# Column-tiled ones-matmuls with a split partial sum for the norm sums of an eight-core decoder trunk

## The chip, the cores and the metric

The kernel runs on all eight cores of one Trainium2 chip: two dies of four cores. Every core works on its own prompt sequence of 2048 tokens and on 16 of the 128 sample tokens, with the same weights. The metric is the device time of the slowest core in microseconds (us). TensorE does the matmuls, VectorE and ScalarE the elementwise work; in the traces each engine goes through its own instructions in the program's order (TensorE's matmuls match the program one for one), and the engines wait for each other by semaphores. SBUF ("MEM" in the profile) is the core's memory, PSUM ("PS") is where TensorE writes: 128 partitions, eight banks of 512 fp32 columns.

Executions of this program come in two states. In the slow one a die shows a lower granted TensorE clock (the share of full speed that the profile says TensorE was given) and the time is some per cent, at most 19%, longer.

## The reference, cut to what matters

```python
def rmsnorm(x, g):
    xf = x.astype(jnp.float32)
    y = xf * lax.rsqrt(jnp.mean(xf * xf, axis=-1, keepdims=True) + EPS)
    return (y * g.astype(jnp.float32)).astype(x.dtype)

def trunk(...):                                    # two layers
    for i in range(DEPTH):
        u = rmsnorm(x, g_mix[i])
        x = x + (pool_mixer(u, ...) if i % 2 == 0 else conv_mixer(u, ...))
        x = x + mem_attend(rmsnorm(x, g_attn[i]), mem_k[i], mem_v[i], w_q[i], w_o[i])
        x = x + sq_relu_mlp(rmsnorm(x, g_ffn[i]), w_up[i], w_down[i])
    return rmsnorm(x, g_final), ...
```

D_MODEL is 1024 and D_FF 4096. The change touches the sum of x*x over 1024 channels in the norms named g_attn, g_ffn and in g_mix of layer 1 (the samples' own 16-column g_ffn sums excepted).

## The kernel before: the parts that matter

Activations lie transposed: channels on the 128 partitions (8 chunks of 128), tokens along the columns. The 2064 tokens of a core are five tiles: four of 416 columns and one of 400 (384 prompt tokens and the 16 samples; without the samples 384 in some stages). A sum over channels is a sum over partitions, which TensorE does with a matrix of ones: eight matmuls, one per channel chunk, accumulate in one PSUM bank, and every row of the bank then holds the full sum.

```python
def norm_r(ti, U, RSTD, n=None):                   # U holds the squares, bf16
    bk = nxt()                                     # next PSUM bank, in rotation
    for c in range(NCH):                           # NCH = 8, ONESB is 128 x 128 ones
        mm(PSv(bk, 0, n), ONESB(), U(c, sl(0, n)), c == 0, c == NCH - 1)
    act(PSv(bk, 0, n), PSv(bk, 0, n), AF.Ln, scale=1.0 / D, bias=EPS)    # ScalarE
    act(RSTD(sl(0, n)), PSv(bk, 0, n), AF.Exp, scale=-0.5)

def norm_s(...):                                   # "gain products", VectorE, eight of them
    for c in cs:
        stt(U(c, ...), X(c, ...), G(c, ...), RSTD(...), ALU.mult, ALU.mult)
```

The helper `norm_b` is `norm_r` followed by `norm_s`. The program has 25 such norms: 1 in the prelude, 6 in each attention phase, 4 and 3 in the two MLPs, 5 in the conv phase. They are put between the chunks of the main work (a chunk is eight matmuls of one tile, 1.41 us at 416 columns), so that ScalarE and VectorE make the next tile's input while TensorE is at this one. The attention phase:

```python
def S(k, mid):                                     # scores of tile k
    for m in range(8):
        bk = nxt()
        ...8 matmuls into bk...
        act(pt(m), PSv(bk, 0, n), AF.Exp, scale=1.0 / 16.0)
        if m % 2 == 1 and m > 1:
            den(m // 2 - 1)                        # a bank, 2 matmuls, Ln, Exp, two products on VectorE
        mid(m)
    den(3)

def O(k, mid):                                     # output of tile k
    for ec in range(8):
        bk = nxt()
        ...8 matmuls into bk, which read pt...
        tt(X(ec, ...), PSv(bk, 0, n), X(ec, ...), ALU.add)
        mid(ec)

def SA(b):                                         # one sample's scores: "dots"
    for h2 in range(2):
        bk = nxt()
        mm(PSv(bk, 0, 512), ..., QS(...), True, True)
        for x in range(2):
            for hh in range(2):
                dot(kv, kv, PSv(bk, hh * 256, (hh + 1) * 256), SS(...))   # VectorE, 0.42 us each

# where things stand in S(k), k > 0 (and in the last O)
if m == 2:  N2b(k + 1) if k + 1 < NT else N3b(0)   # the next norm
if m == 5:  step()                                 # SB: 8 column-tiled matmuls; then SA
if ec == 5: N3b(1)
```

S(k) is followed by O(k-1), and a second sample's step stands at O's chunk ec == 3. Banks rotate over seven in these phases (bank 7 holds the samples' output). Count `nxt()` from SA on: SA takes two banks; chunks m = 6 and 7, den(2), den(3) and ec = 0 take the other five; so O's second and third chunk (ec = 1 and 2) write the two banks that the dots read. They may start only when four, or all eight, of the dots are done.

The softmax here doesn't subtract the row's maximum and nothing guards it: scores larger than these inputs give would overflow.

## Time and profile before

| | before |
|---|---|
| time, median of 3 runs | 1623.22 us (1622.68 to 1623.79) |
| TensorE busy | 1575.0 us, 97% of the span |
| VectorE, ScalarE busy | 854.2 us (53%), 560.8 us (35%) |
| granted TensorE clock | 0.99 |
| norm sums on TensorE | 25 x eight matmuls, 34.8 us |

The first lines are from the profile's page of the kernel before (its slowest core): busy time by engine; the chain of waits that ended last, by engine and by line; and groups of instructions, each with `out<-in` and shape, count, busy us, mean ns of one, then the engine's idle us just before them and what ended most of it. L292 is the plain matmul helper, L327 the helper of the gain products, L304 that of the dots.

```profile
PE 1575.0 (97%) x10104; PEld 906.3 (56%) x10104; DVE 854.2 (53%) x1907; ACT 560.8 (35%) x1054; POOL 113.9 (7%) x245
PE 92%; DVE 2%; ACT 2%; DMA 2%; issue 2%; POOL 0%; DVEq 0%; ACTq 0%; SPq 0%; POOLq 0%
PE PS L292 89%; PE PS L296 2%; DVE MEM L327 1%; ACT MEM L319 1%; PE PS L301 1%; DMA MEM<-gv 1%; DMA MEM<-x 1%; ACT MEM L308 1%; DVE MEM L331 0%; DVE MEM L345 0%; DVE MEM L339 0%; POOL MEM L354 0%; ACT MEM L343 0%; DVEq L1389 0%; ACTq L1389 
L292 PE MATMUL PS<-MEM 128*128 128x416 bf16 (+7 forms) x9024 | 1501.3, 327 | 8.3 <-DVE MEM L345 2.7
L327 DVE SCALAR_TENSOR_TENSOR MEM<-MEM 128x416 bf16<-128x416 f32 (+7 forms) x322 | 176.9, 601 | 126.9 <-ACT MEM L319 108.5
L304 DVE SCALAR_TENSOR_TENSOR MEM<-MEM,PS 128x256 f32<-128x256 f32 x256 | 105.2, 420 | 72.0 <-PE PS L292 49.0
```

TensorE is the limit: 97% busy, 92% of the chain, and before 9024 matmuls it idles 8.3 us in all. VectorE is only half busy *on average*. The next view is VectorE's timeline in one attention tile of layer 1 (core 5; start us, duration us, instruction, count, and in brackets the idle time before it with its cause; the short accumulator reads between the dots are left out).

```profile
1071.76 4.59 DVE L327 SCALAR_TENSOR_TENSOR MEM<-MEM 128x416 bf16<-128x416 f32 x8 [6.28 <-ACT MEM L319]
1076.27 2.09 DVE L331 TENSOR_TENSOR MEM<-MEM 128x416 bf16<-128x416 bf16 x4
1078.27 0.41 DVE L304 SCALAR_TENSOR_TENSOR MEM<-MEM,PS 128x256 f32<-128x256 f32 x1
...
1079.94 0.42 DVE L304 SCALAR_TENSOR_TENSOR MEM<-MEM,PS 128x256 f32<-128x256 f32 x1
...
1081.89 0.42 DVE L304 SCALAR_TENSOR_TENSOR MEM<-MEM,PS 128x256 f32<-128x256 f32 x1
1082.45 2.10 DVE L331 TENSOR_TENSOR MEM<-MEM 128x416 bf16<-128x416 bf16 x4
```

From 1071.76 to 1086 us VectorE hardly rests (no gap is over 0.2 us): eight gain products (4.59 us), four products by a softmax denominator (2.09), eight dots (1078.27 to 1082.31), and so on. So in this stretch it is not half busy, it is full. The same stretch of TensorE, kernel before:

```profile
1075.62 4.05 PE L292 MATMUL PS<-MEM 16*128 16x512 bf16 x21
1079.90 5.96 PE L292 MATMUL PS<-MEM 128*128 128x416 bf16 x33 [0.23 <-ACT MEM L319]
1085.80 0.40 PE L296 MATMUL PS<-MEM 128*16 128x257 bf16 x8
```

The run of 33 matmuls from 1079.90 is the last denominator matmul and O's first four chunks, without a stop. Its third chunk starts 17 matmuls of 176 ns after 1079.90, at 1082.89 us, and the dots that free its bank end at 1082.31. That is a margin of 0.58 us.

The kernel already has column-tiled matmuls, those of SB, each with 16 rows of output. This is their group in the view of groups kept apart by shape, TensorE, kernel before:

```profile
L296 PE MATMUL PS<-MEM 128*16 128x257 bf16 x256 | 12.7, 275 | 2.1 <-ACT MEM L319 2.1
```

### The profile page before, as it was taken

The numbers are of one execution on the slowest core, as the hardware profiler recorded it, in microseconds if no ns is written. First come the engines' busy times: TensorE is split into PE (matmuls) and PEld (weight loads), VectorE is DVE, ScalarE is ACT, GpSimd is POOL, SyncE is SP. The second block draws the span as 40 slices with busy tenths as digits, with TensorE's granted clock in tenths as the row PEclk, the third lists the DMA queues.
The fourth block names the chain that finished last, engine by engine and source line by source line (L and its number), as shares of the span: only waits on it lengthen the run. The fifth ranks groups of instructions, "written<-read, shape, count | busy, mean of one in ns | idle before, by whom it ended". The sixth has DMA issues, their size and how long they took to land.

```text
span 1624.3 us, 28431 instructions; the slowest of 8 cores (1618.2 to 1624.3 us)
## 1 busy us (share of the span) xinstructions
PE 1575.0 (97%) x10104; PEld 906.3 (56%) x10104; DVE 854.2 (53%) x1907; ACT 560.8 (35%) x1054; POOL 113.9 (7%) x245
## 2 busy tenths in 40 slices
PE   4899999999999999999999999999999999999997
PEld 3775555555555556555555555555555555555565
DVE  5666675655444444445666665766455444442235
ACT  4756344541122222222133224433643112213453
POOL 2002121110000000000000001121010000000000
PEclk8899999999999999999999999999999999999999
DMA  9978793575537516066000009694654663000012
GB/s 228 208 116 156 161 183 68 122 148 77 85 66 126 107 24 105 1 104 109 1 1 1 1 1 151 130 201 96 126 118 68 101 105 52 14 1 1 40 64 108
DMA packets 84565, 145.13 MB, mean 89 GB/s; under 512 B 4286, under 2 KB 37310, under 8 KB 84412
## 3 DMA queue, kind: packets, MB, share of 16 engines
q0 software_dynamic: 67568, 84.08, 35.4%
q1 hardware_dynamic: 16860, 59.24, 10.6%
q8 instruction: 84, 1.38, 0.3%
q14 instruction: 53, 0.43, 0.1%
HBM read 212.42 MB, written 14.36 MB: 140 GB/s over the span
## 4 chain that ended last, share of the span: by engine, by line
PE 92%; DVE 2%; ACT 2%; DMA 2%; issue 2%; POOL 0%; DVEq 0%; ACTq 0%; SPq 0%; POOLq 0%
PE PS L292 89%; PE PS L296 2%; DVE MEM L327 1%; ACT MEM L319 1%; PE PS L301 1%; DMA MEM<-gv 1%; DMA MEM<-x 1%; ACT MEM L308 1%; DVE MEM L331 0%; DVE MEM L345 0%; DVE MEM L339 0%; POOL MEM L354 0%; ACT MEM L343 0%; DVEq L1389 0%; ACTq L1389 0%
## 5 line engine op out<-in xcount | busy, mean ns | idle before, releaser
L292 PE MATMUL PS<-MEM 128*128 128x416 bf16 (+7 forms) x9024 | 1501.3, 327 | 8.3 <-DVE MEM L345 2.7
L292 PEld LDWEIGHTS PS<-MEM 128*128 128x128 bf16 (+1 forms) x9024 | 837.3, 98 | 659.8 <-issue 38.5
L319 ACT ACTIVATE MEM<-PS 128x416 f32<-128x416 f32 (+5 forms) x469 | 238.9, 510 | 632.5 <-PE PS L292 622.7
L331 DVE TENSOR_TENSOR MEM<-PS,MEM 128x416 f32<-128x416 f32 (+6 forms) x533 | 297.8, 575 | 264.2 <-PE PS L292 256.1
L331 DVE TENSOR_TENSOR MEM<-MEM 128x416 bf16<-128x416 f32 (+3 forms) x282 | 159.9, 584 | 198.8 <-ACT MEM L319 189.5
L327 DVE SCALAR_TENSOR_TENSOR MEM<-MEM 128x416 bf16<-128x416 f32 (+7 forms) x322 | 176.9, 601 | 126.9 <-ACT MEM L319 108.5
L319 ACT ACTIVATE MEM<-MEM 128x416 bf16<-128x416 f32 (+9 forms) x299 | 185.2, 631 | 146.5 <-DVE MEM L331 111.6
L304 DVE SCALAR_TENSOR_TENSOR MEM<-MEM,PS 128x256 f32<-128x256 f32 x256 | 105.2, 420 | 72.0 <-PE PS L292 49.0
L343 ACT COPY MEM<-PS 128x512 f32<-128x512 f32 (+3 forms) x73 | 39.2, 536 | 129.5 <-PE PS L292 119.1
L296 PE MATMUL PS<-MEM 128*128 128x128 bf16 (+4 forms) x896 | 61.0, 248 | 16.3 <-DVE MEM L339 9.4
L296 PEld LDWEIGHTS PS<-MEM 128*128 128x128 bf16 (+2 forms) x896 | 49.2, 107 | 30.2 <-issue 28.6
L343 ACT CAST MEM<-PS 128x512 bf16<-128x512 f32 (+2 forms) x65 | 35.2, 554 | 68.0 <-PE PS L292 67.3
L345 DVE CAST MEM<-PS 128x512 bf16<-128x512 f32 (+1 forms) x76 | 48.5, 658 | 11.7 <-PE PS L292 11.7
L354 POOL DMA_DIRECT2D MEM<-cv x64 | 47.7, 745 | 13.4 <-PE PS L292 13.4
L319 ACT ACTIVATE PS<-PS 128x416 f32<-128x416 f32 (+3 forms) x67 | 33.2, 495 | 41.5 <-PE PS L292 41.1
L327 DVE SCALAR_TENSOR_TENSOR MEM<-PS,MEM 128x1024 f32<-128x1024 f32 (+1 forms) x17 | 21.8, 1283 | 44.1 <-ACT MEM L319 44.1
L301 PE MATMUL PS<-MEM 128*128 128x128 f32 (+5 forms) x184 | 25.0, 277 | 18.3 <-DMA MEM<-gv 8.4
L351 POOL MEMSET MEM<- 128x4 bf16 (+1 forms) x96 | 15.0, 159 | 359.1 <-PE PS L296 298.5
L301 PEld LDWEIGHTS PS<-MEM 128*128 128x128 f32 (+5 forms) x184 | 20.9, 146 | 21.4 <-issue 19.9
L339 DVE TENSOR_SCALAR MEM<-MEM 128x1024 bf16<-128x1024 f32 (+1 forms) x18 | 17.9, 997 | 24.0 <-ACT MEM L319 24.0
L354 POOL DMA_DIRECT2D MEM<-w_up x36 | 20.6, 582 | 132.5 <-PE PS L292 132.5
L354 POOL DMA_DIRECT2D MEM<-w_down x22 | 13.8, 635 | 202.2 <-PE PS L292 158.1
(28 smaller groups left out, 137.3 us busy)
## 6 DMA issues: line engine op xcount, KB each, us to landing
MEM<-ck SPq DMA_DIRECT2D x64, 512.0 KB, 6.2
MEM<-cv POOLq DMA_DIRECT2D x64, 256.0 KB, 5.8
MEM<-w_down POOLq DMA_DIRECT2D x6, 2048.0 KB, 17.7
MEM<-x SPq DMA_DIRECT2D x16, 512.0 KB, 14.2
MEM<-w_kv POOLq DMA_DIRECT2D x4, 2048.0 KB, 17.9
MEM<-w_o POOLq DMA_DIRECT2D x4, 2048.0 KB, 22.7
MEM<-w_up POOLq DMA_DIRECT2D x32, 256.0 KB, 13.0
MEM<-w_up POOLq DMA_DIRECT2D x4, 2048.0 KB, 17.1
```

The source lines that it names most:

```text
L292: P.add(PE, "c", lambda e, o=out.ap, l=lhsT.ap, r=rhs.ap: e.matmul(out=o, lhsT=l, rhs=r, start=start, stop=stop), [lhsT, rhs], [out])
L296: P.add(PE, "c", lambda e, o=out.ap, l=lhsT.ap, r=rhs.ap: e.matmul(out=o, lhsT=l, rhs=r, start=start, stop=stop, is_transpose=is_transpose ...
L301: P.add(PE, "c", lambda e, o=out.ap, i=in_.ap, d=ident.ap: e.transpose(out=o, in_=i, identity=d), [in_, ident], [out])
L304: P.add(DVE, "c", lambda e, o=out.ap, a=in0.ap, b=in1.ap, c=acc.ap: e.scalar_tensor_tensor(out=o, in0=a, scalar=1.0, in1=b, op0=ALU.mult, ...
L308: P.add(ACT, "c", lambda e, o=out.ap, i=in_.ap, a=acc.ap: e.activation(out=o, in_=i, func=AF.Square, accum_out=a), [in_], [out, acc])
L319: P.add(ACT, "c", lambda e, o=out.ap, i=in_.ap: e.activation(out=o, in_=i, func=func, bias=bias, scale=sc), rd, [out])
L327: P.add(eng, "c", lambda e, o=out.ap, a=in0.ap, b=in1.ap: e.scalar_tensor_tensor(out=o, in0=a, scalar=sc, in1=b, op0=op0, op1=op1), rd, [out])
L331: P.add(eng, "c", lambda e, o=out.ap, a=in0.ap, b=in1.ap: e.tensor_tensor(out=o, in0=a, in1=b, op=op), [in0, in1], [out])
L339: P.add(eng, "c", lambda e, o=out.ap, a=in0.ap: e.tensor_scalar(out=o, in0=a, scalar1=sc, scalar2=None, op0=op0), rd, [out])
L343: P.add(ACT, "c", lambda e, o=out.ap, i=in_.ap: e.copy(out=o, in_=i), [in_], [out])
L345: P.add(eng, "c", lambda e, o=out.ap, i=in_.ap: e.tensor_copy(out=o, in_=i), [in_], [out])
L354: return P.add(q, "d", lambda e, o=out.ap, i=in_.ap: e.dma_start(out=o, in_=i), [in_], [out], chan=chan, after=after)
```

## The change

The intent: a sum needs only one row of output, but `ONESB` of 128 columns makes 128 equal ones. With 32 columns of ones a matmul uses a quarter of the array's columns, and four such matmuls, one per column tile, can run side by side. Eight chunks then take two passes instead of eight. The result of this tiled part (`norm_p`) is four partial sums in four groups of 32 partitions. To add them up and spread them over all partitions, two more matmuls with the full matrix of ones are made (the joining pair, in `norm_r`); a matmul takes bf16 input here, so the partial sums are split in a high half (a copy on ScalarE) and a low half (a subtraction on VectorE). As every partial sum stands in 32 rows, the scale becomes 1/(32 D).

```diff
+    def norm_p(ti, U, RSTD, n=None):
+        n = n or TILES[ti][1]
+        bk = nxt()
+        for i in range(2):
+            for h in range(4):
+                mmx(V(PS[32 * h:32 * h + 32, bk, 0:n], ...), ONESB(sl(0, 32)), U(4 * i + h, sl(0, n)), i == 0, i == 1)
+        hi, lo = [T(RSTD.off + i * n * 2, BF16, [n]) for i in range(2)]
+        cp(hi(), PSv(bk, 0, n), eng=ACT)
+        tt(lo(), PSv(bk, 0, n), hi(), ALU.subtract)
+
     def norm_r(ti, U, RSTD, n=None):
         n = n or TILES[ti][1]
         bk = nxt()
-        for c in range(NCH):
-            mm(PSv(bk, 0, n), ONESB(), U(c, sl(0, n)), c == 0, c == NCH - 1)
-        act(PSv(bk, 0, n), PSv(bk, 0, n), AF.Ln, scale=1.0 / D, bias=EPS)
+        for i in range(2):
+            mm(PSv(bk, 0, n), ONESB(), T(RSTD.off + i * n * 2, BF16, [n])(), i == 0, i == 1)
+        act(PSv(bk, 0, n), PSv(bk, 0, n), AF.Ln, scale=1.0 / (32 * D), bias=EPS)
         act(RSTD(sl(0, n)), PSv(bk, 0, n), AF.Exp, scale=-0.5)
...
# conv phase
-                if c == (4 if ti else 1):
+                if c == (3 if ti else 0):
+                    ...norm_p...
+                if c == (5 if ti else 2):
                     first_norm(1, RSTDQ) if ti == NT - 1 else conv_nB(ti + 1)
...
# S(0)
-                    if m == 4:
+                    if m == 3:
+                        N2p(1)
+                    if m == 5:
                         N2b(1)
# S(k), k > 0
-                if m == 2:
+                if m == 1:
+                    N2p(k + 1) if k + 1 < NT else N3p(0)
+                if m == 3:
                     N2b(k + 1) if k + 1 < NT else N3b(0)
# last O
-            if ec == 5:
+            if ec == 4:
+                N3p(1)
+            if ec == 6:
                 N3b(1)
# MLP: norm_p where norm_b stood, norm_b after the second chunk of what follows
```

So the change also moves things: in the attention and conv phases, where one norm stood, the tiled part now stands one chunk earlier and the joining pair, with the gain products, one chunk later. In the prelude and the MLPs the tiled part keeps the old place and only the joining pair and the gain products move later.

More of the change, by code (lines that the diff above doesn't have):

```diff
@@ L432, in norm_b @@
         norm_s(ti, grow, U, RSTD, n)
+    def norm_p(ti, U, RSTD, n=None):
[3 more added lines that the diff above has]
+            for h in range(4):
+                mmx(V(PS[32 * h:32 * h + 32, bk, 0:n], PSv(bk, 0, 1).ivs, True), ONESB(sl(0, 32)), U(4 * i + h, sl(0, n)), i == 0, i == 1)
+        hi, lo = [T(RSTD.off + i * n * 2, BF16, [n]) for i in range(2)]
+        cp(hi(), PSv(bk, 0, n), eng=ACT)
+        tt(lo(), PSv(bk, 0, n), hi(), ALU.subtract)
     def norm_r(ti, U, RSTD, n=None):
@@ L709, in prelude @@
         extra[11].append(lambda: norm_a(0, BUF[0], parts=2))
-        extra[12].append(lambda: norm_r(0, BUF[0], RSTDE))
+        extra[12].append(lambda: norm_p(0, BUF[0], RSTDE))
+        extra[13].append(lambda: norm_r(0, BUF[0], RSTDE))
         for i in range(4):
@@ L839, in conv_nA, with conv_nP @@
         norm_a(ti, CUT[ti % 2], parts=2)
+    def conv_nP(ti):
+        norm_p(ti, CUT[ti % 2], RSTDQ)
     def conv_nB(ti):
@@ L922, in mid @@
                         conv_nA(ti + 1)
-                if c == (4 if ti else 1):
+                if c == (3 if ti else 0):
+                    if ti == NT - 1:
+                        norm_p(SEQS[1][0], BUF[0], RSTDQ)
+                    else:
+                        conv_nP(ti + 1)
+                if c == (5 if ti else 2):
                     first_norm(1, RSTDQ) if ti == NT - 1 else conv_nB(ti + 1)
@@ L976, in N2a, with N2p @@
             norm_a(seq[k], BT[k % 2])
+        def N2p(k):
+            norm_p(seq[k], BT[k % 2], RSTD)
         def N2b(k):
@@ L1125, in N3a, with N3p @@
             norm_a(ti, BT[1] if ti == 0 else U3[ti], TILES[ti][2])
+        def N3p(ti):
+            norm_p(ti, BT[1] if ti == 0 else U3[ti], RSTDM if ti > 1 else RSTD, TILES[ti][2])
         def N3b(ti):
@@ L1287, in attn_phase @@
                         load(f"dn{l}_{q1 + 1}")
-            if q == 0 and ti + 2 < NT:
-                N3b(ti + 2)
+            nrm = q == 0 and ti + 2 < NT
+            if nrm:
+                N3p(ti + 2)
             yield ("A", j)
@@ L1295, in attn_phase @@
             else:
-                stB(q, ti, j, mid_m)
+                stB(q, ti, j, lambda c: (N3b(ti + 2) if nrm and c == 1 else None, mid_m(c)))
             if ti == NT - 1 and q:
@@ L1345, in build_program @@
         if at == ("A", 18):
+            conv_nP(0)
+        if at == (3, 3):
             conv_nB(0)
```

## The prediction

> **What bounds the kernel now.** TensorE. The page gives it 97% of the span, and the chain that ended last is 92% TensorE. Granted clock 0.99. Followed in program order, the timeline has 25 norm sums of eight ones-matmuls, all at full rate (176 ns apart): 1407 ns at 416 columns (20 of them), 1353 at 400 (3), 1300 at 384 (2). That is 34.8 us, 2.1% of the span, nearly all on the critical path.
>
> **What the change does.** Per norm: eight full matmuls become eight column-tiled ones (two passes of four), a ScalarE copy, a VectorE subtract, and two full matmuls one or two chunks later.
>
> **Cost on TensorE.** The kernel already holds such groups: the sample attention's eight 257-column matmuls in four column tiles, 32 times. The timeline shows four starting 3 to 4 ns apart, the next four 103 ns after (257 columns at full clock take 107 ns). So the tiles do run side by side, as the Trainium skill says ("TensorE: Matmul & The Clock Gate", Part 3). The same groups price the mode change that "TensorEngine Tiling (Array Packing)", Key Properties, calls a drain: 269 instead of 176 ns before the group (+93), 330 ns from the first tiled start to the next full matmul where two passes need 214 (+116), and 10 more on that matmul: about 219 ns a group. At 416 columns I estimate 219 + 2 x 173 for the tiled part and 2 x 176 for the joining pair: 917 ns against 1407, 490 saved (about 464 at 400, 436 at 384). Sum over 25 norms: 12.1 us.
>
> **What is given back (my estimate 2.5 us).**
> - Prelude norm: VectorE sets the pace (a 2.0 us wait on it follows at 93.6 us): 0.5 us.
> - First tile of each attention phase: the partial sums now stand at chunk 3, but the one-piece square on ScalarE (2.9 us) ends only at 115.4 and 998.7 us, where TensorE would get there at 115.0 and 998.1: waits of about 0.4 and 0.7 us. In layer 1 the gain products end just when the sample queries need them (margin before 0.65 us): 0.2 us.
> - Conv phase: the eight gain products (4.6 us of VectorE) come one chunk later, and the chunk-6 gate that frees a bank comes about 0.2 us late per tile; at the last tile 2.3 us of waits for VectorE stay, and little is gained.
> - Elsewhere (MLP, later attention tiles) copy and subtract (0.5 + 0.6 us) fit into the two chunks (2.8 us); I expect no wait before the joining pair.
>
> **Prediction: 1613.8 us** (-0.6%), range 1610 to 1618.5. Faster by over 2%: 0.01; within 2%: 0.98; slower by over 2%: 0.01.
>
> **What would show it.** Tiled groups: four starts a few ns apart, second four about 170 ns later, some 463 ns from the first tiled start to the next full matmul; TensorE busy down by some 10 us; VectorE up by 25 x 0.57 us = 14 us, ScalarE by 25 x 0.5 = 12 us; joining pairs 176 ns apart without wait; new waits of TensorE on ScalarE near 115 and 998 us; the waits at 977 and 985 us moved but not gone.
>
> **What would make it wrong.** Four 416-column streams that don't run side by side (no gain); a larger drain with 32-column tiles; joining pairs that wait for the subtract behind VectorE's queue; bank rotation, shifted by one bank per norm, meeting late VectorE reads.

Its 107 ns and 173 ns are estimates for a pass of 257 and of 416 columns. They can be worked out from the steps between full matmuls in the kernel before: 216 ns at 512 columns less 176 at 416 is 0.417 ns a column. The other few ns of a step are not in them.

## The result, and the profile after

| | before | after |
|---|---|---|
| median of 6 runs each | 1623.82 us (1622.68 to 1625.79) | 1626.09 us (1624.10 to 1626.81) |
| ratio of fast runs, 95% interval | | 1.0012 (0.9999 to 1.0025) |
| TensorE busy, profiled core | 1575.0 us | 1566.1 us |
| VectorE, ScalarE busy | 854.2, 560.8 us | 867.2, 569.6 us |

A ratio here is always the mean time of one kernel's fast runs over that of the other kernel's in the same rounds, so it is not quite the ratio of the medians quoted. The predicted 1613.8 us, and the range 1610 to 1618.5, were missed: the time did not fall. The page of the kernel after, the same lines (its slowest core; line numbers of helpers are the same in both kernels):

```profile
PE 1566.1 (96%) x10154; PEld 891.3 (55%) x10154; DVE 867.2 (53%) x1932; ACT 569.6 (35%) x1079; POOL 114.0 (7%) x245
PE 86%; DVE 6%; issue 3%; ACT 3%; DMA 2%; DVEq 0%; POOL 0%; ACTq 0%; SPq 0%; POOLq 0%
PE PS L292 82%; DVE MEM L327 4%; PE PS L296 3%; ACT MEM L319 1%; DVE MEM L331 1%; DMA MEM<-gv 1%; PE PS L301 1%; DVE MEM L304 1%; DMA MEM<-x 1%; ACT MEM L308 1%; ACT PS L319 0%; DMA y<-MEM 0%; DVE MEM L345 0%; DVE MEM L339 0%; DVEq L1423 0%
L292 PE MATMUL PS<-MEM 128*128 128x416 bf16 (+7 forms) x8874 | 1482.2, 327 | 16.2 <-DVE MEM L304 6.7
L327 DVE SCALAR_TENSOR_TENSOR MEM<-MEM 128x416 bf16<-128x416 f32 (+7 forms) x322 | 176.8, 600 | 49.0 <-ACT MEM L319 43.3
L304 DVE SCALAR_TENSOR_TENSOR MEM<-MEM,PS 128x256 f32<-128x256 f32 x256 | 105.1, 420 | 59.2 <-PE PS L292 36.1
```

TensorE has 8.9 us less work, as intended, and the span has not shrunk. So TensorE waits more: the idle time before its plain matmuls went from 8.3 to 16.2 us, and what ends the largest part of it (6.7 us) is now L304, the samples' dots on VectorE. The chain of waits has VectorE at 6% instead of 2%, most of it in L327, the gain products. Before I look for where, the tiled groups themselves, in the view by shape of the kernel after:

```profile
L296 PE MATMUL PS<-MEM 128*32 128x416 bf16 x160 | 10.7, 344 | 0.0
L296 PE MATMUL PS<-MEM 128*32 128x400 bf16 x24 | 1.6, 336 | 1.0 <-ACT MEM L319 1.0
L296 PE MATMUL PS<-MEM 128*32 128x384 bf16 x16 | 1.0, 331 | 0.0
```

The busy times of 10.7, 1.6 and 1.0 us for 160, 24 and 16 matmuls only add up if four overlap: 160 matmuls in rows of four are 40 passes. The starts in the trace's records confirm it to the nanosecond. This is a list of mine of TensorE's start-to-start steps in ns at one norm of layer 0, kernel after (step into the group, the steps within it, the step of the matmul that follows):

```
in 269 | 3 3 4 176 4 3 3 272 | first tiled start to next full matmul 468 | next matmul 186
joining pair: in 176 | 176 176
```

Predicted were 3 to 4 ns, about 170, "some 463" and a further 10 on the next matmul. So a norm at 416 columns costs TensorE 93 + 468 + 10 + 352 = 923 ns where I said 917, which saves 484 of 1407, and none of the 25 joining pairs waits on any of the six cores with a complete record. The saving exists.

**Where it went.** I matched the trace's matmul records, in program order, with the matmuls of the program, and took the time between the first matmuls of successive stages, the mean of those cores that have a complete record (six of the eight in both kernels). "Nominal" is 490, 464 or 436 ns per norm of the stage. The two attention stages are what the change was supposed to shorten most.

```
us             prelude   attn 0    MLP 0     conv   attn 1    MLP 1    tail      sum
before          106.79   153.55   496.12   221.39   152.88   461.29   30.15  1622.18
after           105.27   154.21   494.14   219.31   158.28   459.97   31.88  1623.06
difference       -1.52    +0.66    -1.98    -2.08    +5.40    -1.32   +1.73    +0.88
nominal          -0.49    -2.91    -1.91    -2.42    -2.91    -1.42    0.00   -12.06
given back                 3.57     0             0.34     8.31     0.10    1.73
```

Between cores these agree within 0.1 us in the middle stages, 1.0 us in the tail. The prelude differs by 1 to 3 us from run to run also where its code is the same (105.83 us in a2 and 103.73 in d2 further down), so no theory is built on its column. ("Tail" is from the last tile's last down-projection to the end.) Both MLPs do what was predicted. The conv phase seems to, but in part a wait has only crossed its border: the last tile's wait for a bank, 1.2 us inside the conv phase before, is now 1.9 us at the second score chunk of layer 1's attention. The two attention phases give back 11.9 us, and the tail gives back 1.7 us although it has no norm of this kind.

**Attention.** This view lists what TensorE waited for in the attention phase of layer 1 on core 5 (us in all, times, the longest), of which I show what it waited for behind the dots; first the kernel before:

```profile
PE PS L292 <- DVE MEM L304: 0.3, 1, 0.3
```

And the same of the kernel after:

```profile
PE PS L292 <- DVE MEM L304: 4.1, 8, 1.1
```

One brief wait for the dots has become eight, of 4.1 us. In the ledger of start-to-start gaps, the waits at O's chunks grew by 3.65 us in layer 0 and by 5.09 us in layer 1. (The start-to-start gap is the better measure: the profile gives a matmul 327 ns on average where a stream starts one every 176 ns, so its modelled ends lie some 150 ns after the next start, and its waits are smaller.) The timeline of VectorE in the same tile as above, kernel after (accumulator reads left out):

```profile
1069.92 1.09 DVE L331 TENSOR_TENSOR MEM<-MEM 128x416 bf16<-128x416 bf16 x2 [3.34 <-ACT MEM L319]
1070.94 4.59 DVE L327 SCALAR_TENSOR_TENSOR MEM<-MEM 128x416 bf16<-128x416 f32 x8
1075.44 1.09 DVE L331 TENSOR_TENSOR MEM<-MEM 128x416 bf16<-128x416 bf16 x2
1076.45 0.41 DVE L304 SCALAR_TENSOR_TENSOR MEM<-MEM,PS 128x256 f32<-128x256 f32 x1
...
1078.12 0.42 DVE L304 SCALAR_TENSOR_TENSOR MEM<-MEM,PS 128x256 f32<-128x256 f32 x1
...
1080.06 0.42 DVE L304 SCALAR_TENSOR_TENSOR MEM<-MEM,PS 128x256 f32<-128x256 f32 x1
1080.41 0.08 DVE L304 DVE_READ_ACCUMULATOR MEM<-MEM,PS 128x1 f32 x1
```

TensorE's timeline of the same stretch, kernel after:

```profile
1076.53 1.74 PE L292 MATMUL PS<-MEM 128*128 128x416 bf16 x9 [0.23 <-ACT MEM L319]
1078.69 1.57 PE L292 MATMUL PS<-MEM 128*128 128x416 bf16 x8 [0.42 <-DVE MEM L304]
1080.64 2.97 PE L292 MATMUL PS<-MEM 128*128 128x416 bf16 x16 [0.38 <-DVE MEM L304]
```

Read both against the start of the last denominator matmul, just ahead of O (1079.90 us before, 1076.53 us after):

```
us from that matmul                 before     after
gain products start                  -8.14     -5.59
first dot starts                     -1.63     -0.08
fourth dot ends (frees ec = 1)       +0.46     +2.01
ec = 1 starts                        +1.58     +2.16
eighth dot ends (frees ec = 2)       +2.41     +3.95
ec = 2 starts                        +2.99     +4.11
```

In the kernel before O's chunks start on TensorE's own pace. In the kernel after each starts 0.15 to 0.16 us after the dot that frees its bank. The gain products came 2.55 us later, measured against O: the joining pair is a chunk later, its Ln and Exp then stand behind a denominator's on ScalarE and the gain products behind two of that denominator's products on VectorE (the line at 1069.92), and TensorE reaches O 0.49 us sooner. Two products less then stand between the gain products and the dots, so the dots come 1.55 us later (-0.08 against -1.63). VectorE is busy from the gain products to the last dot in both kernels, with gaps of 0.2 us at most, so nothing absorbs it. The slack was 0.43 us (0.58 less the 0.15 us that pass between a dot's end and the chunk's start); O loses 1.12 us in two waits. The norm saved 0.49 us and lost 1.12: this tile is 0.63 us slower, not 0.49 faster (28.28 us against 27.65 from its last denominator matmul to the next tile's). The other later tiles of layer 1 lost 1.2 to 1.4 us at these two waits.

**The rest of layer 1's attention.** There are 1.9 us more of wait at the second score chunk of the first tile, where VectorE still does the conv phase's last tile (1.2 us of it stood inside the conv phase before), 0.8 us at the tiled group of the first tile (the wait on ScalarE predicted as 0.7), and 0.5 us at the sample queries.

**Tail.** Here the output tokens are normed and written by blocks of 128: TensorE turns a block, VectorE scales it (L327, 128 x 1024) into one of two buffers, from which a DMA writes it to y. A third block needs the first buffer, so it waits for that write. VectorE's timeline in the tail has this line for the fourth block in the kernel before (core 5):

```profile
1606.51 1.28 DVE L327 SCALAR_TENSOR_TENSOR MEM<-PS,MEM 128x1024 f32<-128x1024 f32 x1 [0.81 <-ACT MEM L319]
```

And this for the same block in the kernel after (core 6):

```profile
1606.90 1.28 DVE L327 SCALAR_TENSOR_TENSOR MEM<-PS,MEM 128x1024 f32<-128x1024 f32 x1 [2.71 <-DMA y<-MEM]
```

The block waits 2.71 us for `y<-MEM` in the kernel after; before it waited for ScalarE only. Both kernels issue the write at the same place (9.0 us into the tail), but it lands 2.7 us later before, and 4.5 to 5.0 us later after. What differs is a block of TensorE's instructions. They are fetched in blocks of one packet each (16,384 bytes in the trace), and the page counts the packets of the queue that brings them (packets, MB, share). From the page of the kernel before:

```profile
q8 instruction: 84, 1.38, 0.3%
```

And of the kernel after:

```profile
q8 instruction: 85, 1.39, 0.4%
```

84 packets for 21,572 TensorE instructions in the trace became 85 for 21,724 (21,572 / 84 is 257, so a packet holds about 256 of them). The change added 152 instructions, so every fetch after them comes at another point. In the kernel after one starts 10.0 to 11.0 us into the tail, 1.0 to 2.0 us after that write is issued; in the kernel before they come in its first 2.1 us or 15.9 us or more into it, and there is none there (one core excepted, where a fetch at 18.6 hit a write issued at 17.6 that then took 4.6 us, and the tail took 30.7 us instead of 30.0). The Trainium skill ("Runtime: NRT & Kernel Launch", Instruction fetch mechanics) gives the same block of 256 instructions and 16 KiB, and calls its cost "mostly hidden". It is hidden from TensorE here (moving the fetches, a4 below, changed no stage before the tail by more than 0.3 us, the prelude aside). It was not hidden from another DMA.

### The profile page after: what moved, and what is told of

Read it like the earlier page. It is cut to its first block, busy times and chain, and to the rows that moved or that the text cites. A ratio compares the mean times of both kernels' runs of the same rounds, so it can differ in the third digit from the quotient of the medians.

```text
span 1624.8 us, 28505 instructions; the slowest of 8 cores (1621.9 to 1624.8 us)
## 1 busy us (share of the span) xinstructions
PE 1566.1 (96%) x10154; PEld 891.3 (55%) x10154; DVE 867.2 (53%) x1932; ACT 569.6 (35%) x1079; POOL 114.0 (7%) x245
## 3 DMA queue, kind: packets, MB, share of 16 engines
q1 hardware_dynamic: 16860, 59.24, 10.6%
## 4 chain that ended last, share of the span: by engine, by line
PE 86%; DVE 6%; issue 3%; ACT 3%; DMA 2%; DVEq 0%; POOL 0%; ACTq 0%; SPq 0%; POOLq 0%
PE PS L292 82%; DVE MEM L327 4%; PE PS L296 3%; ACT MEM L319 1%; DVE MEM L331 1%; DMA MEM<-gv 1%; PE PS L301 1%; DVE MEM L304 1%; DMA MEM<-x 1%; ACT MEM L308 1%; ACT PS L319 0%; DMA y<-MEM 0%; DVE MEM L345 0%; DVE MEM L339 0%; DVEq L1423 0%
## 5 line engine op out<-in xcount | busy, mean ns | idle before, releaser
L292 PE MATMUL PS<-MEM 128*128 128x416 bf16 (+7 forms) x8874 | 1482.2, 327 | 16.2 <-DVE MEM L304 6.7
L292 PEld LDWEIGHTS PS<-MEM 128*128 128x128 bf16 (+1 forms) x8874 | 819.3, 98 | 665.2 <-issue 61.6
L331 DVE TENSOR_TENSOR MEM<-PS,MEM 128x416 f32<-128x416 f32 (+6 forms) x558 | 311.9, 575 | 316.6 <-PE PS L292 259.6
L327 DVE SCALAR_TENSOR_TENSOR MEM<-MEM 128x416 bf16<-128x416 f32 (+7 forms) x322 | 176.8, 600 | 49.0 <-ACT MEM L319 43.3
L304 DVE SCALAR_TENSOR_TENSOR MEM<-MEM,PS 128x256 f32<-128x256 f32 x256 | 105.1, 420 | 59.2 <-PE PS L292 36.1
L296 PE MATMUL PS<-MEM 128*128 128x128 bf16 (+6 forms) x1096 | 74.2, 265 | 16.6 <-DVE MEM L339 9.1
L343 ACT CAST MEM<-PS 128x512 bf16<-128x512 f32 (+6 forms) x90 | 47.6, 537 | 83.0 <-PE PS L292 67.2
L296 PEld LDWEIGHTS PS<-MEM 128*128 128x128 bf16 (+3 forms) x1096 | 52.1, 105 | 39.2 <-issue 37.7
L327 DVE SCALAR_TENSOR_TENSOR MEM<-PS,MEM 128x1024 f32<-128x1024 f32 (+1 forms) x17 | 21.8, 1283 | 45.9 <-ACT MEM L319 43.2
L319 ACT ACTIVATE PS<-PS 128x416 f32<-128x416 f32 (+2 forms) x67 | 33.2, 495 | 32.8 <-PE PS L292 32.8
```

The lines of the kernel that those rows point to most:

```text
L292: P.add(PE, "c", lambda e, o=out.ap, l=lhsT.ap, r=rhs.ap: e.matmul(out=o, lhsT=l, rhs=r, start=start, stop=stop), [lhsT, rhs], [out])
L296: P.add(PE, "c", lambda e, o=out.ap, l=lhsT.ap, r=rhs.ap: e.matmul(out=o, lhsT=l, rhs=r, start=start, stop=stop, is_transpose=is_transpose ...
L304: P.add(DVE, "c", lambda e, o=out.ap, a=in0.ap, b=in1.ap, c=acc.ap: e.scalar_tensor_tensor(out=o, in0=a, scalar=1.0, in1=b, op0=ALU.mult, ...
L319: P.add(ACT, "c", lambda e, o=out.ap, i=in_.ap: e.activation(out=o, in_=i, func=func, bias=bias, scale=sc), rd, [out])
L327: P.add(eng, "c", lambda e, o=out.ap, a=in0.ap, b=in1.ap: e.scalar_tensor_tensor(out=o, in0=a, scalar=sc, in1=b, op0=op0, op1=op1), rd, [out])
L331: P.add(eng, "c", lambda e, o=out.ap, a=in0.ap, b=in1.ap: e.tensor_tensor(out=o, in0=a, in1=b, op=op), [in0, in1], [out])
```

## Experiments

The theories: **L** (lateness): the gain products come a chunk later, push the dots, and O's second and third chunk wait for their banks. Against it stand: the extra bank that `norm_p` takes from the rotation, and costs of the tiled mode itself beyond its group. **F** (fetch): the tail's loss comes from where an instruction fetch falls. Against it stands: the tail is longer because of what the change does to VectorE or ScalarE. Ledger numbers below are made as above, from each run's profile; "medians" are of timed runs. All eleven kernels gave correct results.

### a1_sooner: the change with attention's norms one chunk sooner

```diff
 # the kernel after; S(0), S(k), last O
-                    if m == 5:
+                    if m == 4:
                         N2b(1)
-                if m == 1:
+                if m == 0:
                     N2p(k + 1) if k + 1 < NT else N3p(0)
-                if m == 3:
+                if m == 2:
                     N2b(k + 1) if k + 1 < NT else N3b(0)
-            if ec == 4:
+            if ec == 3:
                 N3p(1)
-            if ec == 6:
+            if ec == 5:
                 N3b(1)
```

The joining pairs stand where the full sums stood before, and the tiled parts one chunk ahead of their place in the change (the first tile's excepted). The extra bank, the tiled mode and the extra copies stay.

> The changed kernel with only the attention norms moved: the joining pair stands where the single norm sum stood before (chunk 2, and chunk 4 of a phase's first tile, chunk 5 of the last output tile), the column-tiled sums two chunks ahead of it (one for the first tile). Tiles, copy, subtract and extra bank all stay. Theory L (the gain products start a chunk later, so the sample's dot products free their two PSUM banks late and the output matmuls wait): the waits of TensorE before the second and third output chunk fall from 9.0 us a core to under 1 us; attention phase of layer 0 from 154.2 to about 151 us, of layer 1 from 158.3 to about 152 us; whole kernel about 9 us faster than the changed one, ratio to before about 0.995. Rival W (the added copy, subtract and third bank per norm load VectorE and the banks): both phases stay within 1 us of the changed kernel.

Measured: ratio 0.9956 (0.9932 to 0.9979); two fast runs of 1616.29 and 1618.77 us against a median of 1625.04 (its other two runs were slow, 1659.91 and 1915.38). Attention took 150.87 and 154.18 us instead of 154.21 and 158.28. The waits at O's chunks are 0.3 us a core, from 9.0. VectorE's timeline of a1 in the tile of layer 1 looked at above:

```profile
1061.50 4.59 DVE L327 SCALAR_TENSOR_TENSOR MEM<-MEM 128x416 bf16<-128x416 f32 x8 [3.28 <-ACT MEM L319]
1068.01 0.41 DVE L304 SCALAR_TENSOR_TENSOR MEM<-MEM,PS 128x256 f32<-128x256 f32 x1
```

TensorE's, kernel a1, the same tile:

```profile
1069.56 5.96 PE L292 MATMUL PS<-MEM 128*128 128x416 bf16 x33 [0.23 <-ACT MEM L319]
```

The gain products stand 8.06 us ahead of the last denominator matmul again, the first dot 1.55 us, and 33 matmuls run without a stop. With the extra bank and the tiled mode both still there, neither can have made the waits. Theory L holds. Layer 1 missed the 152 us or so that I would have liked: the first tile, whose squares come late, now has 1.5 us of wait at its joining pair, which has one chunk only for copy and subtraction, and the 1.9 us at the second score chunk stayed.

### a2_before_late: the kernel before, with its norms one chunk later

```diff
 # the kernel before; no tiled sums
-                    if m == 4:
+                    if m == 5:
                         N2b(1)
-                if m == 2:
+                if m == 3:
                     N2b(k + 1) if k + 1 < NT else N3b(0)
-            if ec == 5:
+            if ec == 6:
                 N3b(1)
```

Lateness alone, without anything else of the change.

> The kernel before, with its eight full matmuls per norm, but the attention norms moved to where the changed kernel joins (chunk 3, chunk 5 of the first tile, chunk 6 of the last output tile). No tile, no copy, no subtract. Theory L: the waits before the second and third output chunk appear here too, about 1 us a tile; attention phase of layer 0 from 153.5 to about 157 us, of layer 1 from 152.9 to about 158 us; total about 8 us slower than before (ratio 1.005). Rival W: both phases within 0.5 us of before.

Measured: ratio 1.0030 (1.0008 to 1.0053), median 1629.71 us (one slow run left out). Attention 154.37 and 154.83 us: +0.82 and +1.95. The waits at O's second and third chunks are 3.8 us in eight places (0.5 us of it stood in one place in the kernel before). So lateness alone makes the kernel slower in the same place, but less than I expected. The same tile's timelines give the reason: against the last denominator matmul the first dot starts at -0.80 us in a2, between -1.63 (before) and -0.08 (after), and O waits once, 0.40 us. So the 1.55 us of the kernel after are three things. 0.83 is lateness alone. 0.48 is the saving itself: the last denominator matmul starts 14.20 us after the tile's first score matmul instead of 14.68 (the matmul before it), and where VectorE sets the pace this comes back as wait. The remaining 0.24 I put down to the tiled group's new place (read from a2's and the kernel after's traces, not tested by a run of its own): it stands ahead of chunks m = 2 and 3, so den(0) comes 0.57 us later in S than in a2, and the norm's Ln, behind den(0)'s Ln and Exp on ScalarE, 0.25 us later.

### a3_before_pad and a4_after_pad: moving the instruction fetches

```diff
+    for _ in range(76):        # a3, on the kernel before; a4: 52, on the kernel after
+        mm(PSv(7, 0, 4), ONESB(), ONESB(sl(0, 4)), True, True)
```

These matmuls of four columns run at the start, while TensorE waits for data, and do nothing but count: two instructions each. a3 brings the kernel before to the instruction count of the kernel after (21,725 against 21,724). a4 adds 105 to the kernel after, so that the fetches come about as many instructions apart from the tail as before (257 more than in the kernel before, a block and one).

> The kernel before, with 76 four-column matmuls at the very start, where TensorE waits for its first load; they move every later TensorE instruction by as many places as the change does (153 against 152), so that the fetches of TensorE's instructions fall as in the changed kernel. Theory F (the last stretch is longer because a fetch of TensorE's instructions[...] now falls on a write of y and holds it up): the stretch from the last MLP tile's down-projection to the end grows from 30.15 to about 31.9 us. Rival R (the bank rotation, or late VectorE work, of the changed kernel): it stays at 30.15. All other stages unchanged within 0.3 us, the prelude aside.

> The changed kernel with 52 four-column matmuls at the very start: 257 places in all against the kernel before, one place more than a whole 256-instruction fetch, so that the fetches fall in the last stretch as before. Theory F: the last stretch falls from 31.9 to about 30.2 us, the kernel is about 1.7 us faster than the changed one. Rival R: stays at 31.9.

Measured: a4's tail is 30.05 us, 1.83 less than that of the kernel after; its fetches are at 1.2 to 1.3 and 15.7 to 16.4 us, and its first three writes land in 2.6 to 2.8 us. The rest of its ledger is that of the kernel after within 0.3 us a stage, as far as the prelude is left out. a3's tail is 30.62 us, expected was that of the kernel after, 31.9: a miss in size. Its fetch fell at 7.2 to 8.3 us, earlier than meant, and hit the write issued at 6.2 us instead (4.5 to 5.2 us to land), which the tail can bear better. This is a list of mine from the trace's DMA records: the tail of single cores, the fetches in it, and issue and landing time of the first three writes to y (us into the tail).

```
kernel  core  tail    fetch starts   writes to y: issued (landed after)
before  1     30.00    1.3, 16.4     6.2 (2.7)   8.9 (2.7)  10.7 (2.7)
after   1     31.87   10.0, 21.6     6.2 (2.7)   9.0 (4.7)  10.8 (4.1)
after   3     31.26   10.1, 21.3     6.2 (2.6)   9.0 (4.5)  10.8 (3.9)
a3      1     30.39    7.2, 25.0     6.2 (4.5)   9.0 (2.9)  12.2 (2.6)
a3      2     30.00   11.9           6.2 (2.7)   9.0 (2.7)  10.8 (5.1)
a4      1     29.99    1.2, 15.7     6.2 (2.6)   8.9 (2.7)  10.7 (2.7)
```

Theory F holds: the same arithmetic with another instruction count restores the tail (a4), and in every row where a fetch starts about a microsecond after one of these writes was issued, that write is the late one. (In the kernel after the next write, issued 0.8 us behind the fetch's start, is late as well.) b2 below shows the same within one execution, without padding: on three cores the fetch starts at 9.9 us and the tail takes 31.1 to 32.0 us, on three it starts at 8.6 or 11.7 us and the tail takes 30.0. Total times, 1625.48 us (ratio 1.0004, 0.9989 to 1.0019) and 1625.80 (1.0008, 0.9993 to 1.0024), do not separate 1 or 2 us; for these two the verdict rests on the tails in the profiles.

### b1_placed, b2_adjacent, b3_one_half: with the joining pairs at the old places in attention and conv

b1 puts the joining pair and gain products where the full sums stood in the conv phase too, leaves the old eight matmuls in the first tile of layer 1 whose squares come late, and squares and sums layer 0's first tile a chunk sooner. The MLPs' joining pairs stay where the change put them. b2 also moves 13 of the tiled groups of attention and MLP right in front of a sample's column-tiled matmuls, so that two groups share one change of mode. b3 is b1 without the low half of the split: no subtraction, one joining matmul.

```diff
 # b1, on a1; conv phase, and S(0)
-                if c == (5 if ti else 2):
+                if c == (4 if ti else 1):
                     first_norm(1, RSTDQ) if ti == NT - 1 else conv_nB(ti + 1)
-                        N2b(1)
+                        N2b(1) if l == 0 else N2o(1)          # N2o: the old eight matmuls
 # b2, on b1; inside O(k - 1), before the sample's step there
+                    if ec == 3 and k + 2 <= NT:
+                        N2p(k + 2) if k + 2 < NT else N3p(0)
 # b3, on b1; norm_p and norm_r
-        cp(hi(), PSv(bk, 0, n), eng=ACT)
-        tt(lo(), PSv(bk, 0, n), hi(), ALU.subtract)
+        cp(T(RSTD.off, BF16, [n])(), PSv(bk, 0, n), eng=ACT)
-        for i in range(2):
-            mm(PSv(bk, 0, n), ONESB(), T(RSTD.off + i * n * 2, BF16, [n])(), i == 0, i == 1)
+        mm(PSv(bk, 0, n), ONESB(), T(RSTD.off, BF16, [n])(), True, True)
```

> The changed kernel with every joining pair put back where the single sum stood before (attention as in a1_sooner; conv phase chunk 4 instead of 5, chunk 1 for the first tile), the first tile of layer 0 squared a chunk earlier and summed at chunk 2, and the first tile of layer 1 left with its eight full matmuls (its square ends too late for tiles). Theory L: all waits that the change brought go. Stage by stage against the kernel before: attention layer 0 about -2.9 us (150.6), MLP 0 -1.9, conv -2.4 (219.0, the 1.9 us wait of the next attention phase's second chunk gone), attention layer 1 -2.4 (150.4), MLP 1 -1.4; the last stretch 30 to 32 by where an instruction fetch falls. Together 10 to 11 us, ratio 0.9935. If something else than the placement holds the conv phase up (rival W), conv and the wait after it stay as in the changed kernel.

> b1_placed with the tiled norm sums of most attention and MLP tiles moved directly before the sample's own column-tiled matmuls, so that TensorE enters and leaves the tiled mode once for both. If the mode change costs what the traces say (93 ns in, about 109 ns out), each of the about 11 pairs saves about 0.2 us: 2 us in all against b1_placed. If the two groups' tile shapes (32 against 16 columns) force a change between them, nothing.

> b1_placed without the second bf16 half: no subtract, one joining matmul. Each of 24 norms saves one 416-column matmul (0.176 us), 4.2 us against b1_placed, VectorE 14 us less busy; the result rounds the partial sums to bf16 once, about 0.1% in the norm's scale, and should still be correct within the tolerance, though it is a coarser kernel.

```
us              prelude   attn 0    MLP 0     conv   attn 1    MLP 1    tail   ratio to before (95%)
b1_placed        104.32   151.22   494.17   222.46   149.86   459.92   30.40   0.9951 (0.9938 to 0.9965)
b2_adjacent      103.78   150.70   493.14   223.70   148.78   459.06   30.76   0.9946 (0.9933 to 0.9958)
b3_one_half      104.38   150.28   493.45   221.26   149.80   459.46   29.90   0.9929 (0.9915 to 0.9943)
```

Medians 1617.67, 1615.43 and 1612.84 us against 1624.98 (two of b1's seven runs were slow). Attention and MLP came within 0.6 us of what I expected: layer 1's attention went from 158.28 to 149.86. The conv phase is a miss: 222.46 us where I expected 219.0. Its waits are 3.8 us a core: 0.3 to 0.4 us once in each of the first four tiles, at the fifth chunk of the first and at the eighth of the others, and 2.2 us at the eighth chunk of the last, all for the product with the gate on VectorE that frees their bank. VectorE takes 3.6 us for a conv chunk when it does not wait for TensorE (0.9 of it is a wait for ScalarE), a conv chunk on TensorE is 4.22 us, and the gain products' 4.6 us come in one block on top. In the kernel before it just kept up: TensorE waits there in one place only, 1.2 us at the last tile. With 0.48 us less on TensorE per tile it does not, and the saving comes back as wait once more. The kernel after has the same small waits, 0.3 to 0.4 us a tile, and its 219.31 us are shorter mainly because the last tile's wait stands behind the border there: 1.9 us at the second score chunk of layer 1's attention, which b1 does not have. So in both places of the join the conv phase's saving is nearly lost.

One thing the ledger hides: after the 2.2 us wait three of b1's six cores, and after a 2.5 us wait five of b2's, ran about ten matmuls at 333 ns instead of 169 (granted clock 0.50 for 3.0 to 3.3 us, where it was 1.00 before). This adds some 1.6 us to the conv phase of those cores and shortens a later wait in layer 1's attention by 1.2 to 1.4 us; b1's cores differ by 1.7 us there for this reason.

b2 against b1 in the stages where the groups became neighbours: -0.52, -1.03, -1.08 and -0.86 us (attention 0, MLP 0, attention 1, MLP 1), 3.5 us for 13 pairs (counted from the program's order); I expected about 2 us for 11. Not all of this is the mode: one sample's step in each MLP waits less, and in attention 1 the slow matmuls above move waits across the border (conv and attention 1 together take 372.3 us in b1 and 372.5 in b2). The starts in the trace give it directly: a group of 416 columns and a sample's group take 994 ns apart (93 + 468 + 10 and 93 + 330) and 781 as neighbours, with 166 ns from the last start of one group to the first of the next. That is 0.21 us a pair, in agreement with the 93 ns into a group and 99 + 10 after it. b3 against b1 is -3.8 us in the ledger's sum (expected 4.2; none of b3's cores had the slow matmuls): about the low half's price. It is a different rounding, so I don't put it forward as a replacement.

### c1_spread, c2_before_spread: gain products of the conv phase dealt out over chunks 4 to 7

```diff
 # c1 on b2, c2 on the kernel before; c1 also has 58 small matmuls at the start
-                if c == (4 if ti else 1):
-                    first_norm(1, RSTDQ) if ti == NT - 1 else conv_nB(ti + 1)
+                c1, w = (1, 2) if not ti else (4, 3) if ti == NT - 1 else (4, 2)
+                ...
+                if c == c1:
+                    norm_r(tj, ut, RSTDQ)
+                if c >= c1 and (c - c1) * w < NCH:
+                    norm_s(tj, grow, ut, RSTDQ, cs=range((c - c1) * w, min(NCH, (c - c1 + 1) * w)))
```

If a block of 4.6 us is too much for VectorE at one chunk, two products per chunk should fit.

> b2_adjacent with the conv phase's eight gain products dealt out over four chunks (two a chunk; three for the last tile) instead of one block, the first tile of layer 0 summed at chunk 3 instead of 2, and 58 four-column matmuls at the start that put the instruction fetches of the last stretch where they fall in the kernel before. Theory L, that a block of gain products (4.6 us) makes VectorE free the conv banks late, since a conv chunk leaves it 0.7 us to catch up: the conv phase's waits fall from 5.8 us to under 1.5, the phase from 223.7 to about 219 us; attention layer 0 from 150.7 to about 150; last stretch 30.0; in all about 16 us faster than before, ratio 0.990. Rival W (the extra bank per norm is what holds the conv phase up): conv stays above 222.

> The kernel before, with only the conv phase's gain products dealt out as in c1_spread; no tiles. It shows how much of c1_spread's gain comes from the dealing out alone: the two waits at 977 and 985 us (2.3 us together) should go or shrink, conv about -1.2 us, attention layer 1 about -1 us; other stages unchanged. If it gains 5 us or more, the tiles have little part in what c1_spread gains in the conv phase.

Measured: both worse. Conv took 233.02 us in c1 and 233.96 in c2, ratios 1.0011 (0.9997 to 1.0024) and 1.0092 (1.0077 to 1.0108), medians 1627.97 and 1641.03 against 1626.07. TensorE's waits for gain products in most of the conv phase (up to 965 us), c1, slowest core:

```profile
PE PS L292 <- DVE MEM L327: 9.6, 6, 3.2
```

The last two products now come after the last chunk, and the next tile's first chunk needs them: up to 3.2 us at a time. From start to start this is 3.4 to 3.7 us a tile, 10.6 us a core in three tiles (10.0 in c2). After most of these waits TensorE then ran six to fifteen matmuls at 347 ns instead of 176 (on one core of c1 at 888 us the granted clock is 0.50 for 3.1 us): in c1 another 2.7 to 5.8 us a core. The traces show that these slow stretches follow waits of 2.2 us and more, and not after every one (three of b1's cores had none after the same wait as the others); no run here tests what decides it or sets the length. My mistake, and the same one as in the prediction: I dealt with when VectorE has room, not with when its result is needed.

### d1_spread_early, d2_before_early: the same, one chunk sooner

```diff
 # d1 on b2, d2 on the kernel before; d1 also has 57 small matmuls at the start
-                if c == 2:                  # squares of the next tile
+                if c == 1:
-                if c == (3 if ti else 0):   # tiled sums (d1 only)
+                if c == (2 if ti else 0):
+                c1 = 3 if ti else 1         # joining pair (d2: full sum) after chunk c1
+                if c == c1:
+                    norm_r(tj, ut, RSTDQ)
+                if c1 <= c < c1 + 4:        # two gain products after each of four chunks, done by chunk 6
+                    norm_s(tj, grow, ut, RSTDQ, cs=(2 * (c - c1), 2 * (c - c1) + 1))
```

> c1_spread with the conv phase's norm moved a chunk earlier: squares at chunk 1, tiled sums at chunk 2, joining pair at chunk 3, two gain products after each of chunks 3 to 6 (first tile: chunks 1 to 4), so that the last two products are done before the next tile's first chunk reads them. In c1_spread and c2_before_spread that reading waited about 3 us a tile for products dealt out to the last chunk. Theory L: no such wait, and none of the bank waits; conv phase about 218 us, the two waits at the last tile gone or small, attention layer 1 about 148.5 us, last stretch 30.0; in all about 18 us faster than before, ratio 0.989. Rival W (the extra bank per norm holds the conv phase up): conv stays above 222.

> The kernel before, without tiles, with the conv phase's squares, sums and gain products placed as in d1_spread_early. It shows what the placing alone is worth: the waits of the last tile (2.3 us) go or shrink, conv about -1.2, attention layer 1 about -1 us, all else unchanged; total about 2 us faster than before. The difference of the two kernels in the conv phase, about 2.4 us, is then what five tiled norms save where nothing takes it back.

```
us                   prelude   attn 0    MLP 0     conv   attn 1    MLP 1    tail      sum
d2_before_early       103.73   153.55   496.12   220.23   153.86   461.29   30.44  1619.23
d1_spread_early       103.48   149.92   493.15   217.84   151.70   458.97   29.99  1605.05
d1 less d2             -0.25    -3.63    -2.97    -2.39    -2.16    -2.32   -0.45   -14.18
```

d1: ratio 0.9913 (0.9897 to 0.9929), median 1610.37 us against 1625.13 for the kernel before in the same rounds (one slow run left out). It is the best version that keeps both halves, and beats both kernels. d2: ratio 1.0006 (0.9988 to 1.0024): the new places by themselves are worth nothing. The difference of the two in the conv phase is -2.39 us, where five tiled norms are nominally worth 2.42; but 1.1 us of it comes back behind the border, where the wait at layer 1's first score chunk is 2.1 us in d1 and 1.0 in d2. On d1's page (slowest core):

```profile
PE 1561.3 (97%) x10193; PEld 896.9 (56%) x10209; DVE 866.0 (54%) x1931; ACT 570.6 (35%) x1078; POOL 113.8 (7%) x245
PE 93%; DMA 2%; DVE 2%; ACT 2%; issue 1%; POOL 0%; DVEq 0%; ACTq 0%; SPq 0%; POOLq 0%
L292 PE MATMUL PS<-MEM 128*128 128x416 bf16 (+8 forms) x8921 | 1477.7, 326 | 11.3 <-DVE MEM L327 2.9
```

TensorE is 93% of the chain again and busy 97%; the idle time before its plain matmuls is 11.3 us, 16.2 in the kernel after and 8.3 before. The whole gain is some 15 us by the medians where I expected about 18. Not all is won: attention of layer 1 took 151.70 us where I expected 148.5. About 2.2 us of wait stand at its first score chunks: VectorE ends the conv phase late, and the wait has moved over the stage's border, as it did in d2 (+0.98 us there). I have not found a place for the last conv tile's work that avoids it; that stays open.

## Why the prediction was wrong

**Right.** TensorE bounds the kernel. Tiles run side by side, the mode change costs what SB's groups showed, a norm saves 0.48 us for 0.49 predicted: 468 ns from the first tiled start to the next full matmul against 463. TensorE's busy time fell by 8.9 us ("some 10"), VectorE's rose by 13.0 (14), ScalarE's by 8.8 (12, too high). The waits on ScalarE near 115 and 998 us came (0.51 and 0.79 us with 0.09 us of mode change in each, for 0.4 and 0.7). MLP 0 and 1 shortened by 1.98 and 1.32 us for a nominal 1.91 and 1.42. In the last conv tile the waits stayed, as 1.9 and 1.3 us for the 1.2 and 1.1 before.

**Wrong.** The step that failed is: "Elsewhere (MLP, later attention tiles) copy and subtract fit into the two chunks (2.8 us); I expect no wait before the joining pair." Each word of it is true: the joining pair does not wait. But I asked only about the wait *before* the join, and took "given back" to end there. In the later attention tiles the join brings the gain products with it, 4.6 us of VectorE, and they went a chunk later into a queue that is full up to the dots, whose last bank O's third chunk needs 0.58 us after the dots end. What the runs showed in place of "no wait" is up to two waits at O in each of seven tiles, 3.65 us in layer 0 and 5.09 in layer 1 (8.7 of the 14 us below). The term "given back (my estimate 2.5 us)" measured about 14: 3.57 + 8.31 in attention (I had 1.3 there, all in first tiles; 1.9 of the 8.31 comes from the conv phase's last tile), 0.3 in conv, 0.1 in the second MLP, and 1.7 in the tail. Without the prelude the nominal saving is 11.57 us; 14.0 less 11.57 is 2.4 us slower. The ledger without its prelude column says 2.4 as well, and the medians differ by 2.27. I named "bank rotation ... meeting late VectorE reads" as a way to be wrong, but by a shift of the rotation. a1 has the same shift and no wait. It was the reads that were late.

**Not foreseen at all.** The tail's 1.7 us, from the place of an instruction fetch (theory F; a4 takes it away).

**Open.** The exact size of a3's tail could not be set beforehand, as its fetch fell elsewhere than planned. The prelude's 1 to 3 us between runs are not explained, nor what decides whether a core's clock drops to half after a wait. How d1's remaining 2 to 3 us at the start of layer 1's attention could be had is not known.

## What to carry to other kernels

When a change moves work to a later slot, follow it past its own wait: list what stands behind it in the queue of the engine that it lands on, and which buffer *that* frees, and set the margin there (here 0.58 us) against the delay (here 1.55 us). A saving on the bounding engine counts only where the engine behind it has slack in that stretch; where it is busy without a gap, as VectorE was in the attention tiles and in the conv phase, the saving comes back as wait until that engine's work is moved sooner or spread to where both room and deadline allow (d1, in part). And before a loss of a microsecond or two in an untouched stage is explained by engine work, look whether the change in instruction count has moved an instruction fetch onto a transfer that something waits for.

## What the Trainium skill lacked or had wrong

- "TensorEngine Tiling (Array Packing)", Key Properties, says that a change of tiling mode drains TensorE and gives no price. Here it cost 93 ns going in and about 99 + 10 ns coming out (the 272 ns from the last tiled start less a pass of 173, and 10 on the next matmul), some 0.2 us a group, with 32-column tiles as with the samples' 16; two groups side by side shared it and saved 0.21 us a pair (b2).
- "TensorE: Matmul & The Clock Gate", Part 1, says that dense matmuls on three cores of a die bring a 13/16 clock. With all eight cores dense for 1.6 ms the granted clock here was 0.99 in fast runs, and no profile used here showed 0.81. Slow runs do: in the two slowest (1915.38 and 1932.63 us) the cores of one die had means of 0.81 to 0.83, which is about 13/16, and in the other eleven means of 0.84 to 0.98. So here it is a state of some executions, on one die, and not the rule under load.
- Same page, Back-to-back issue gap: it gives about 131 ns per matmul at N = 512 as sustained. Streams of 416 columns went at 176 ns and of 512 columns at 216 ns each here, which is the same page's isolated formula (416 / 2.4 + 2.5 = 175.8 and 512 / 2.4 + 2.5 = 215.8, estimates from the page). The 4 ns between starts of tiles (Part 3) agrees: 3 to 4 ns.
- "Runtime: NRT & Kernel Launch", Instruction fetch mechanics, has the block size right (about 256 instructions and 16,384 bytes a packet here) but not the side effect: a fetch that starts 1 to 2 us after a 512 KB write is issued made the write land in 4.5 to 5.2 us instead of 2.6 to 2.8, and so cost the end of the kernel 1.7 us.
